# Layer 0's V phase: a block's row sums issued between the product G and its low part gl on VectorE

## The chip, the core and the metric

The kernel runs on one core of a Trainium2 chip. The metric is the device time of one launch in microseconds (us), taken as the median of several runs. TensorE (PE) multiplies matrices, with its weight loads shown as PEld; VectorE is DVE, ScalarE is ACT, GpSimd is POOL, and SyncE (SP) only issues transfers here.

## The reference

Two layers of a diffusion trunk over 256 context tokens and 256 latent tokens of width 1024. Each layer is a mixer (attention in layer 0, pooling and a recurrence in layer 1) followed by a PEER expert block. What matters here is the last lines of that block:

```python
def peer_ffn(h, wq, subkeys, u, v):
    ...
        eidx = jnp.take_along_axis(cidx, pos, axis=-1)
        g = jax.nn.softmax(top_s, axis=-1)
        act = jax.nn.gelu(jnp.einsum('td,thkd->thk', xc, u[eidx]).astype(jnp.float32), approximate=False)
        coef = (g * act).astype(xc.dtype)
        return jnp.einsum('thk,thkd->td', coef, v[eidx])
```

Each token chooses 8 heads x 16 experts = 128 rows of `v` out of 16384 and adds them up with its own weights.

## The kernel before

The kernel does not gather the rows for most tokens. It multiplies densely: the 16384 experts are 128 blocks of 128, the routing weights stand in a table `Wd` that is zero for experts not chosen, and the activations of all experts stand in `Gd`. The **V phase** of layer 0 is the loop `for j in range(NK)` (128 blocks) in `peer`. For block j it does this:

- SP fetches the block's 128x1024 rows of `v` into `wr` (4 buffers), the activations into `gr` (3 buffers), and every 8th block the weights of 8 blocks at once into `wb` (1536 KB, 2 buffers).
- `load_split` cuts `wr` into a rounded high part `whi` (ACT, L364) and the rest `wlo` (DVE, L365), 3 buffers each.
- DVE multiplies weights and activations to `G` (L1107, 128x384, 2 buffers). `split` makes the high part `gh` on ACT (L352) and the low part `gl` on DVE (L353), which reads `G` and `gh`. There are 3 buffers of each.
- PE adds three products (gh·whi, gl·whi, gh·wlo) for each of 8 column pieces into `y` (L1167): 24 matmuls of 384 columns.

Only 384 of the 512 tokens go this way in layer 0. The last 128 tokens go through `sparse`: POOL gathers, for each of their 128 choices, one row of `v` per token (128x1024, L1004) and one activation per token (L1009), into a ring of 10 row buffers, and DVE adds the row times its weight into `ysp` (L1024). Below, one such addition is a **row sum**. `sparse` is a generator; the loop over blocks advances it, by the `while done < ...` lines, so that the 128 row sums spread over the blocks 15 to 119: mostly one in a block, two in 23 of them.

DVE and POOL run in the order in which the code is written (`manual_schedule`). The orders of PE, ACT and SP come from a scheduler that plans each instruction by its own estimate of when the inputs are ready.

Of the kernel before, what the change touches and what calls it, by code (L numbers as in the profile page):

```python
# [21 lines left out]
P = 128  # L22
# [19 lines left out]
S0 = 14  # L42
S1 = 119
# [66 lines left out]
class Trunk:  # L110
# [918 lines left out]
    def peer(self, l, t0, extra=None):  # L1029
        nc, a = self.nc, self.a  # L1030
        n = T - t0
        nd = n if l else n - P
        Wd = self.dram.tile([nd // TG, P, NK, TG], F32, name=f"Wd{l}")
        Gd = self.Gd[l]
        with ExitStack() as es:
            ps = self.pool(es, f"psU{l}", 2, PSUM)
            rp = self.pool(es, f"route{l}")
            if l:
                hq = self.pool(es, "hq", side="right")
                h = [hq.tile([P, C, n], F32R, name=f"h{x}") for x in range(2)]  # L1040
            else:
                h = self.hf
            r = self.routing(l, ps, rp, h, n, Wd)
            if l == 0:
                xt = [self.new_tot() for _ in range(2)]
                self.sx = {"w": xt[0][:, :P], "g": xt[0][:, P:], "e": xt[1][:, :P].bitcast(U32),
                           "v": xt[1][:, P:].bitcast(U32)}
                self.tok = rp.tile([P, 1], F32, name="tok")
                nc.gpsimd.iota(self.tok, pattern=[[0, 1]], base=0, channel_multiplier=1,
                               allow_small_or_imprecise_dtypes=True)  # L1050
            next(r)
            if extra:
                self.mp = rp
                self.cb = rp.tile([P, 2, D], F32, tag="skey", name="cb")
                self.mod_load()
            es.enter_context(self.tc.manual_schedule(engines={mybir.EngineType.PE, mybir.EngineType.DVE}))
            total = (nd // P) * TOT + (n - nd) // P * TOTS
            st = [0.0, 0.0]
            pet = NK - (XU / 2 + 5 if l == 0 else 8)

            def pace(pe):
                st[1] += pe
                while st[0] * pet < total * st[1]:
                    c = next(r, None)
                    if c is None:
                        break
                    st[0] += c

            for j in range(NK):
                part = l == 0 and j < XU  # L1070
                self.u_step(ps, l, j, h, LC if part else 0, n, mid=lambda: pace(0.25 if part else 0.5))
                pace(0.25 if part else 0.5)
                if extra and j >= M0:
                    next(extra, None)
            for _ in r:
                pass
            if extra:
                for _ in extra:
                    pass
        es = ExitStack()  # L1080
        if l == 0:
            self.rec_alloc()
        ps = self.pool(es, f"psV{l}", 1, PSUM)
        vp = self.pool(es, f"vph{l}", 2)
        if l == 0:
            sp = self.sparse(vp)
            done = -1
            extra = self.v_extra()
        y = [ps.tile([P, n], F32, name=f"y{d}") for d in range(C)]
        last = []  # L1090
        vm = ExitStack()
        if l == 0:
            rc = self.rec_consts()
            vm.enter_context(self.tc.manual_schedule(engines={mybir.EngineType.DVE, mybir.EngineType.Pool}))
        for j in range(NK):
            if j % JB == 0:
                wb = vp.tile([P, nd // TG, JB, TG], F32, tag="wb", name="wb")
                nc.sync.dma_start(wb, Wd[:, :, j:j + JB, :].rearrange("g i j t -> i g j t"))
            g = vp.tile([P, nd], F32, tag="gr", name="gr", bufs=3)
            nc.sync.dma_start(g, Gd[j][:, :nd])  # L1100
            if l == 0 and j < XU:
                with self.tc.issue_after(self.gel.ins) if VG <= j < 6 else ExitStack():
                    nc.scalar.activation(g[:, :LC], g[:, :LC], AF.Gelu)
            with self.tc.issue_after(self.gel.ins) if j in VB else ExitStack():
                w = self.load_split(a["vT"][l, j])
            G = vp.tile([P, nd], F32, tag="G", name="G")
            nc.vector.tensor_tensor(G.rearrange("p (g t) -> p g t", t=TG), wb[:, :, j % JB, :],  # L1107
                                    g.rearrange("p (g t) -> p g t", t=TG), op=OP.mult)
            gh = vp.tile([P, nd], F32R, tag="gh", name="gh", bufs=3)
            gl = vp.tile([P, nd], F32R, tag="gl", name="gl", bufs=3)  # L1110
            if j < VD:
                nc.vector.tensor_copy(gh, G)
                nc.vector.tensor_tensor(gl, G, gh.bitcast(F32), op=OP.subtract)
            else:
                self.split(gh, gl, G)
            v = (w, gh, gl)
            if j < NK - KT:
                for d in range(C):
                    self.v_mm(y[d], v, d, 0, nd, j == 0)
            else:  # L1120
                last.append(v)
            if l == 0:
                if j in RC:
                    next(rc, None)
                if j == 40:
                    for d in range(C):
                        nc.vector.memset(y[d][:, nd:], 0.0)
                while done < (j - S0) * P / (S1 - S0):
                    if next(sp, 0) == 0:
                        break  # L1130
                    done += 1
                if j >= X0:
                    next(extra, None)
        if l == 0:
            for _ in sp:
                pass
            vm.close()
            for _ in extra:
                pass
        if l == 0:  # L1140
            self.bridge(es, y, last)
        else:
            self.tot = self.new_tot()
            for d in range(C):
                for v in last:
                    self.v_mm(y[d], v, d, 0, n)
                self.v_add(l, y[d], d, 1, 0)
                self.sq_acc(self.tot, d, LC, T)
            es.close()
# [444 lines left out]
```

## Time and profile before

| | |
|---|---|
| median of 3 runs | 2862.78 us (2859.86 to 2864.86) |
| the profiled execution | 2869.51 us, span 2867.7 us |
| mean granted TensorE clock | 0.966 of 2.4 GHz |
| PE busy | 2652.9 us, 93% of the span |
| DVE busy | 2098.2 us, 73% |
| bytes read and written by DMA | 631.58 MB, mean 220 GB/s |

The span runs from the first to the last instruction of the profiled execution; its own time is 1.8 us longer, and 6.7 us above the median of the runs. The blocks 15 to 119 of layer 0's V phase lie from about 1318 to 1824 us of the span. A busy share is a mean over stages that are limited by different things, so each stage has to be read by itself.

### The profile page before, as it was taken

Reading aid. Unit: us, or ns where it says so; the run is one execution under the profiler, and the core shown is the slowest. Engines: PE = TensorE matmul, PEld = TensorE weight load, DVE = VectorE, ACT = ScalarE, POOL = GpSimd, SP = SyncE. Lnnn points to the kernel's source line nnn. Section 1 sums busy time; section 2 is a strip of 40 time slices with the busy share of each in tenths; the row PEclk is TensorE's granted clock in tenths of the full one; section 3 lists DMA queues with packets and bytes.
Section 4 is the critical chain, followed back from the end, with each engine's and each line's share of the span. In section 5 each row is a group of like instructions: output and inputs, shape, how many; then the busy total and the mean of one; then the engine's idle time right before and its main releaser. Section 6 shows DMA issues by size and latency. Waiting matters only on the chain.

```text
span 2867.7 us, 45935 instructions
## 1 busy us (share of the span) xinstructions
PE 2652.9 (93%) x17403; PEld 2402.6 (84%) x17403; DVE 2098.2 (73%) x3697; ACT 1172.5 (41%) x1945; POOL 1285.1 (45%) x730
## 2 busy tenths in 40 slices
PE   8879999999899999999899998986999799999997
PEld 3667898987777777788888888976999799999997
DVE  5898764749958879226877777779839939677776
ACT  3444433433233333333333333354545445455544
POOL 3433430754444444445667665035387587600000
PEclk9989999999999999999999999998999999999999
DMA  7342262556547666667999998513477667898885
GB/s 258 125 133 74 95 211 81 192 190 242 197 169 269 228 227 221 196 235 259 316 324 340 342 322 305 190 50 111 157 217 242 210 209 240 289 302 294 293 287 167
DMA packets 296269, 631.58 MB, mean 220 GB/s; under 512 B 28480, under 2 KB 166384, under 8 KB 290416
## 3 DMA queue, kind: packets, MB, share of 16 engines
q1 hardware_dynamic: 226704, 468.03, 50.0%
q0 software_dynamic: 28768, 109.75, 10.3%
q10 hardware_dynamic: 40576, 50.87, 4.9%
q8 instruction: 136, 2.23, 0.3%
q14 instruction: 85, 0.70, 0.1%
HBM read 535.28 MB, written 93.33 MB: 219 GB/s over the span
## 4 chain that ended last, share of the span: by engine, by line
PE 47%; DVE 33%; issue 7%; DMA 6%; POOL 4%; ACT 3%; SPq 0%; ACTq 0%; DVEq 0%; POOLq 0%
PE y L1167 16%; PE pu L373 6%; PE pu L375 6%; PE pu L374 6%; DVE mj L166 4%; DVE A L973 3%; DVE B L975 3%; DVE B L976 3%; DVE wlo L365 3%; DVE B L974 2%; DVE ysp L1024 2%; POOL wlo L365 2%; PE pq L373 1%; PE pq L375 1%; PE pq L374 1%
## 5 line engine op out<-in xcount | busy, mean ns | idle before, releaser
L365 POOL TENSOR_TENSOR wlo<-wr,whi 128x1024 fp32r<-128x1024 f32 x306 | 800.7, 2623 | 729.3 <-ACT whi L364 591.9
L364 ACT ACTIVATE whi<-wr 128x1024 fp32r<-128x1024 f32 x575 | 609.1, 1060 | 937.6 <-PE pu L374 493.1
L1167 PE MATMUL y<-gh,whi 128*128 128x256 f32 (+1 forms) x2072 | 630.2, 310 | 41.4 <-ACT gh L352 40.1
L1167 PE MATMUL y<-gl,whi 128*128 128x256 f32 (+1 forms) x2072 | 642.6, 310 | 6.0 <-DVE gl L353 4.8
L1167 PE MATMUL y<-gh,wlo 128*128 128x256 f32 (+1 forms) x2072 | 637.7, 308 | 0.0
L365 DVE TENSOR_TENSOR wlo<-wr,whi 128x1024 fp32r<-128x1024 f32 x291 | 356.0, 1224 | 239.0 <-ACT whi L364 212.9
L1167 PEld LDWEIGHTS y<-gh,whi 128*128 128x128 f32 x2072 | 391.0, 190 | 52.6 <-ACT gh L352 50.5
L373 PE MATMUL pu<-hh,whi 128*128 128x512 f32 (+1 forms) x1024 | 395.7, 386 | 20.9 <-ACT gel L538 20.9
L1167 PEld LDWEIGHTS y<-gl,whi 128*128 128x128 f32 x2072 | 393.7, 190 | 15.3 <-DVE gl L353 12.8
L1167 PEld LDWEIGHTS y<-gh,wlo 128*128 128x128 f32 x2072 | 394.1, 190 | 0.0
L375 PE MATMUL pu<-hh,wlo 128*128 128x512 f32 (+1 forms) x1024 | 386.5, 377 | 3.7 <-POOL wlo L365 3.7
L374 PE MATMUL pu<-hl,whi 128*128 128x512 f32 (+1 forms) x1024 | 384.5, 375 | 0.0
L373 PE MATMUL pu<-h,whi 128*128 128x256 f32 x1024 | 296.1, 289 | 15.2 <-ACT whi L364 15.2
L375 PE MATMUL pu<-h,wlo 128*128 128x256 f32 x1024 | 290.6, 284 | 7.4 <-POOL wlo L365 7.4
L374 PE MATMUL pu<-h,whi 128*128 128x256 f32 x1024 | 289.6, 283 | 0.0
L373 PEld LDWEIGHTS pu<-hh,whi 128*128 128x128 f32 x1024 | 196.1, 191 | 53.4 <-ACT gel L538 22.7
L375 PEld LDWEIGHTS pu<-hh,wlo 128*128 128x128 f32 x1024 | 195.7, 191 | 41.0 <-POOL wlo L365 4.9
L374 PEld LDWEIGHTS pu<-hl,whi 128*128 128x128 f32 x1024 | 196.6, 192 | 31.8
L353 DVE TENSOR_TENSOR gl<-G,gh 128x384 fp32r<-128x384 f32 (+1 forms) x250 | 127.7, 511 | 119.6 <-ACT gh L352 119.6
L373 PEld LDWEIGHTS pu<-h,whi 128*128 128x128 f32 x1024 | 195.8, 191 | 15.4 <-ACT whi L364 15.4
L166 DVE SCALAR_TENSOR_TENSOR mj<-wm,cb 128x1024 bf16<-128x1024 f32 x128 | 206.6, 1614 | 1.0 <-DMA wm<-in_wmodT 0.8
L375 PEld LDWEIGHTS pu<-h,wlo 128*128 128x128 f32 x1024 | 195.2, 191 | 8.9 <-POOL wlo L365 8.9
(378 smaller groups left out, 4900.0 us busy)
## 6 DMA issues: line engine op xcount, KB each, us to landing
wr<-in_uT SPq DMA_DIRECT2D x278, 512.0 KB, 4.4
wr<-in_vT SPq DMA_DIRECT2D x256, 512.0 KB, 5.0
wm<-in_wmodT SPq DMA_DIRECT2D x80, 512.0 KB, 4.0
Wd<-stg POOLq DMA_DIRECT2D x40, 1024.0 KB, 7.0
Gd<-gel ACTq DMA_DIRECT2D x106, 256.0 KB, 2.4
wb<-Wd SPq DMA_DIRECT2D x16, 1536.0 KB, 12.5
gr<-Gd SPq DMA_DIRECT2D x128, 192.0 KB, 6.2
Gd<-gel ACTq DMA_DIRECT2D x172, 128.0 KB, 3.8
```

Source lines behind the costliest of these rows:

```text
L166: x = nc.vector.scalar_tensor_tensor(j, rs[i], 1.0, self.cb[:, s], op0=OP.mult, op1=OP.mult, accum_out=self.mv[l][n // C][:, n % C, s:s + 1])
L353: self.nc.vector.tensor_tensor(lo, x, hi.bitcast(F32), op=OP.subtract)
L364: nc.scalar.activation(hi, r, AF.Copy)
L365: (lo_engine or nc.vector).tensor_tensor(lo, r, hi.bitcast(F32), op=OP.subtract)
L373: nc.tensor.matmul(out, whi[:, s], hh[:, c, t0:t1], start=c == 0, stop=False)
L374: nc.tensor.matmul(out, whi[:, s], hl[:, c, t0:t1], start=False, stop=False)
L375: nc.tensor.matmul(out, wlo[:, s], hh[:, c, t0:t1], start=False, stop=c == C - 1)
L973: V.tensor_tensor(Av, io, x[0], op=OP.is_equal)
L974: V.tensor_tensor(Bv[1], io, x[1], op=OP.is_equal)
L975: V.tensor_tensor(Bv[0], Bv[1], x[2], op=OP.mult)
L976: V.tensor_tensor(Bv[1], Bv[1], x[3], op=OP.mult)
L1167: nc.tensor.matmul(y[:, n0:n1], w[:, s], g[:, n0:n1], start=first and x == 0, stop=False, skip_group_check=True)
```

## The change

The lines that advance the row sums move up. Before, a block's row sums were issued after `G`, `gl` and the block's matmuls. Now they are issued right after `G`, before `gh` and `gl`.

```diff
             G = vp.tile([P, nd], F32, tag="G", name="G")
             nc.vector.tensor_tensor(G.rearrange("p (g t) -> p g t", t=TG), wb[:, :, j % JB, :],
                                     g.rearrange("p (g t) -> p g t", t=TG), op=OP.mult)
+            while l == 0 and done < (j - S0) * P / (S1 - S0):
+                if next(sp, 0) == 0:
+                    break
+                done += 1
             gh = vp.tile([P, nd], F32R, tag="gh", name="gh", bufs=3)
             gl = vp.tile([P, nd], F32R, tag="gl", name="gl", bufs=3)
...
                 if j == 40:
                     for d in range(C):
                         nc.vector.memset(y[d][:, nd:], 0.0)
-                while done < (j - S0) * P / (S1 - S0):
-                    if next(sp, 0) == 0:
-                        break
-                    done += 1
                 if j >= X0:
                     next(extra, None)
```

The numbers of instructions stay the same on every engine. DVE's order for the blocks 59 and 60 of the loop before (G_14046 is block 59's product, G_14087 block 60's; `tot` is a small product that prepares the weights of eight row sums):

```order
L365 TENSOR_TENSOR wlo_14043<-wr_14040,whi_14042 128x1024
L1107 TENSOR_TENSOR G_14046<-wb_13910,gr_14038 128x384
L353 TENSOR_TENSOR gl_14049<-G_14046,gh_14048 128x384
L1024 SCALAR_TENSOR_TENSOR ysp_12095<-hl_12092,tot_4165,ysp_12095 128x1024
L365 TENSOR_TENSOR wlo_14084<-wr_14081,whi_14083 128x1024
L1107 TENSOR_TENSOR G_14087<-wb_13910,gr_14079 128x384
L353 TENSOR_TENSOR gl_14090<-G_14087,gh_14089 128x384
L1024 SCALAR_TENSOR_TENSOR ysp_12095<-hl_12092,tot_4165,ysp_12095 128x1024
L1019 TENSOR_TENSOR tot_4165<-tot_4165 128x8
L1024 SCALAR_TENSOR_TENSOR ysp_12095<-hl_12092,tot_4165,ysp_12095 128x1024
L365 TENSOR_TENSOR wlo_14129<-wr_14126,whi_14128 128x1024
```

The same two blocks on DVE now:

```order
L365 TENSOR_TENSOR wlo_14043<-wr_14040,whi_14042 128x1024
L1107 TENSOR_TENSOR G_14046<-wb_13910,gr_14038 128x384
L1024 SCALAR_TENSOR_TENSOR ysp_12067<-hl_12064,tot_4165,ysp_12067 128x1024
L353 TENSOR_TENSOR gl_14052<-G_14046,gh_14051 128x384
L365 TENSOR_TENSOR wlo_14084<-wr_14081,whi_14083 128x1024
L1107 TENSOR_TENSOR G_14087<-wb_13910,gr_14079 128x384
L1024 SCALAR_TENSOR_TENSOR ysp_12067<-hl_12064,tot_4165,ysp_12067 128x1024
L1019 TENSOR_TENSOR tot_4165<-tot_4165 128x8
L1024 SCALAR_TENSOR_TENSOR ysp_12067<-hl_12064,tot_4165,ysp_12067 128x1024
L353 TENSOR_TENSOR gl_14097<-G_14087,gh_14096 128x384
L365 TENSOR_TENSOR wlo_14129<-wr_14126,whi_14128 128x1024
```

The row sums moved from behind `gl` to in front of it; nothing else on DVE changed place.

The scheduler's plan for ACT changed with it. ACT's order around block 59 before (whi_14083 belongs to block 60, whi_14128 to block 61, gh_14048 to block 59):

```order
L352 ACTIVATE gh_14007<-G_14005 128x384
L364 ACTIVATE whi_14083<-wr_14081 128x1024
L352 ACTIVATE gh_14048<-G_14046 128x384
L364 ACTIVATE whi_14128<-wr_14126 128x1024
L352 ACTIVATE gh_14089<-G_14087 128x384
```

ACT's order there now (gh_14051 belongs to block 59, whi_14083 to block 60 as before):

```order
L364 ACTIVATE whi_14042<-wr_14040 128x1024
L352 ACTIVATE gh_14051<-G_14046 128x384
L364 ACTIVATE whi_14083<-wr_14081 128x1024
L352 ACTIVATE gh_14096<-G_14087 128x384
L364 ACTIVATE whi_14128<-wr_14126 128x1024
```

Before, the next block's `whi` stood ahead of this block's `gh` in 100 of the 105 blocks 15 to 119; now it does in 18 of them (26 to 31, 41 to 48, and four near 105).

PE's order at the start of block 79 before (gh_14890, gl_14891 and whi_14884 are block 79's; y0 to y7 are the column pieces):

```order
L1167 MATMUL y0_11482<-gh_14890,whi_14884 128x384
L1167 MATMUL y1_11483<-gh_14890,whi_14884 128x384
L1167 MATMUL y2_11484<-gh_14890,whi_14884 128x384
L1167 MATMUL y3_11485<-gh_14890,whi_14884 128x384
L1167 MATMUL y0_11482<-gl_14891,whi_14884 128x384
L1167 MATMUL y0_11482<-gh_14890,wlo_14885 128x384
```

PE's order there now (gh_14893 and gl_14894 are block 79's):

```order
L1167 MATMUL y0_11482<-gh_14893,whi_14884 128x384
L1167 MATMUL y0_11482<-gl_14894,whi_14884 128x384
L1167 MATMUL y0_11482<-gh_14893,wlo_14885 128x384
L1167 MATMUL y1_11483<-gh_14893,whi_14884 128x384
L1167 MATMUL y1_11483<-gl_14894,whi_14884 128x384
L1167 MATMUL y1_11483<-gh_14893,wlo_14885 128x384
```

Matmuls that need only `gh` were pulled ahead of the first one that needs `gl` in 33 of the 105 blocks; now they are in 6, and elsewhere `gl` is needed by the block's second matmul. SP's order of transfers differs only by swaps of neighbours. Outside the blocks 15 to 119 all orders are as before.

## Rows read from the trace of the kernel before

**Rows 1.** Page, part 4: shares of the chain that ended last, by engine.

```profile
PE 47%; DVE 33%; issue 7%; DMA 6%; POOL 4%; ACT 3%; SPq 0%; ACTq 0%; DVEq 0%; POOLq 0%
```

**Rows 2.** Stretch, us; PE, PEld, DVE, ACT, POOL busy; clock; DMA share; GB/s.

```profile
1318.00:1340.00 22.00, 18.41 (x96) 17.83 (x96) 12.82 (x18) 7.60 (x13) 9.44 (x8) 0.92 0.78 255
1340.00:1500.00 160.00, 147.36 (x806) 142.79 (x804) 128.07 (x180) 52.12 (x68) 106.85 (x81) 0.97 0.93 317
1500.00:1730.00 230.00, 211.48 (x1165) 202.22 (x1166) 180.14 (x213) 77.16 (x100) 155.84 (x119) 0.99 0.97 333
1730.00:1800.00 70.00, 62.30 (x332) 59.61 (x331) 54.98 (x62) 24.04 (x30) 30.17 (x18) 0.95 0.92 309
1800.00:1824.00 24.00, 23.67 (x136) 23.03 (x135) 20.06 (x25) 8.35 (x11) 0.00 (x0) 1.00 0.63 216
```

**Rows 3.** DVE's timeline: start, us, engine, line; a block with one sum, one with two.

```profile
1408.41 1.21 DVE L365 TENSOR_TENSOR wlo<-wr,whi 128x1024 fp32r<-128x1024 f32 x1
1409.55 0.55 DVE L1107 TENSOR_TENSOR G<-wb,gr 128x384 f32<-128x384 f32 x1
1410.75 0.60 DVE L353 TENSOR_TENSOR gl<-G,gh 128x384 fp32r<-128x384 f32 x1 [0.65 <-ACT gh L352]
1411.27 1.27 DVE L1024 SCALAR_TENSOR_TENSOR ysp<-hh,tot,ysp 128x1024 f32<-128x1024 f32 x1
1412.46 1.21 DVE L365 TENSOR_TENSOR wlo<-wr,whi 128x1024 fp32r<-128x1024 f32 x1
...
1415.32 2.59 DVE L1024 SCALAR_TENSOR_TENSOR ysp<-hh,tot,ysp 128x1024 f32<-128x1024 f32 x2
1417.83 1.22 DVE L365 TENSOR_TENSOR wlo<-wr,whi 128x1024 fp32r<-128x1024 f32 x1
```

**Rows 4.** Groups of DVE, 1318 to 1824: line, count, busy, mean ns, idle before.

```profile
L353 DVE TENSOR_TENSOR gl<-G,gh 128x384 fp32r<-128x384 f32 x105 | 64.2, 611 | 96.0 <-ACT gh L352 96.0
```

**Rows 5.** PE's timeline, 21 matmuls to the end of block 58; start of block 59.

```profile
1532.71 0.34 PE L1167 MATMUL y<-gh,whi 128*128 128x384 f32 x1
...
1536.17 0.34 PE L1167 MATMUL y<-gh,wlo 128*128 128x384 f32 x1
1537.62 0.44 PE L1167 MATMUL y<-gh,whi 128*128 128x384 f32 x1 [1.10 <-ACT gh L352]
```

**Rows 6.** ACT's timeline at the same place.

```profile
1530.93 0.53 ACT L352 ACTIVATE gh<-G 128x384 fp32r<-128x384 f32 x1 [2.53 <-DVE G L1107]
1536.09 1.06 ACT L364 ACTIVATE whi<-wr 128x1024 fp32r<-128x1024 f32 x1 [4.64 <-DMA wr<-in_vT]
1537.06 0.51 ACT L352 ACTIVATE gh<-G 128x384 fp32r<-128x384 f32 x1
```

**Rows 7.** Waits of ACT, 1318 to 1824: us in total, times, longest.

```profile
ACT whi L364 <- PE y L1167: 66.0, 63, 5.3
ACT whi L364 <- DMA wr<-in_vT: 64.7, 24, 6.9
```

**Rows 8.** DMA issues, 1318 to 1824: count, KB each, median us to landing.

```profile
wr<-in_vT SPq DMA_DIRECT2D x105, 512.0 KB, 5.6
gr<-Gd SPq DMA_DIRECT2D x105, 192.0 KB, 6.8
wb<-Wd SPq DMA_DIRECT2D x13, 1536.0 KB, 13.1
```

**Rows 9.** Short stretches, columns as in rows 2.

```profile
1534.00:1540.00 6.00, 4.75 (x26) 4.17 (x25) 3.30 (x5) 2.53 (x3) 2.75 (x4) 1.00 1.03 393
1544.00:1548.00 4.00, 3.56 (x20) 2.95 (x19) 3.35 (x5) 1.47 (x2) 3.39 (x3) 1.00 0.74 217
1560.00:1568.00 8.00, 8.00 (x48) 8.00 (x47) 7.20 (x8) 2.67 (x4) 5.18 (x5) 1.00 1.10 331
1604.00:1618.00 14.00, 12.73 (x73) 12.28 (x72) 11.17 (x15) 4.64 (x6) 10.28 (x9) 1.00 1.04 394
```

## The prediction

> **What bounds it now.** The page's chain gives DVE a third of the span [rows 1], although its busy share is lower than PE's; so there are stages in which DVE is waited for. I looked for them in the blocks with row sums, cut into stretches [rows 2]. PE is busy for 147.4 of 160 us, 211.5 of 230 and 62.3 of 70, and for 23.7 of 24 at the end, so it waits here and hardly there. The transfers stand at a share of 0.93, 0.97 and 0.92. DVE's timeline [rows 3] shows the order wlo, G, a hole of 0.65 us before gl, gl, the row sum, the next wlo. From wlo to wlo a block takes 1412.46 - 1408.41 = 4.05 us with one sum and 1417.83 - 1412.46 = 5.37 us with two. There are 82 blocks of the first kind and 23 of the second (counted from the loop's numbers), so DVE needs (82 x 4.05 + 23 x 5.37) / 105 = 4.34 us a block. PE goes from one matmul to the next in (1536.17 - 1532.71) / 20 = 0.173 us [rows 5], so a block's 24 cost it 4.15 us. DVE is therefore the slower of the two, and PE starts a block when DVE and ACT hand over its gh.
>
> A second limit lies close. Of the 96.0 us that DVE waits for gh before the 105 gl [rows 4], 105 x 0.65 = 68 us are the usual hole and 28 us are longer waits. One is block 59's: ACT stands for 4.64 us with block 60's whi, whose wr has not landed, and runs block 59's gh only after it [rows 6]; PE idles 1.10 us [rows 5]. ACT waited 24 times, 64.7 us, for a wr that was late [rows 7]. wr lands a median 5.6 us after its issue, the weights wb take 13.1 us [rows 8], and they come every 8 blocks, about as far apart as these stalls.
>
> **The change, part by part.**
>
> *DVE's hole.* The sum moves into the wait for gh. After G it runs for 1.27 us [rows 3], longer than the 0.65 us that gh needs, so gl finds gh ready. A block falls to 3.40 us with one sum, 4.72 with two, 3.69 on the average: below PE's 4.15. DVE is no longer the bound; by DVE and PE alone the stage would go at 4.15 us a block.
>
> *gl comes later.* After G, gl now starts 1.3 us on (one sum) or 2.6 us (two), not 0.65 us, and PE's second matmul wants it. This costs nothing if DVE runs ahead of PE. How far it can: whi has 3 buffers, so block j+1's whi starts when PE has ended block j-2. Then come whi 1.06 us, wlo 1.21, G 0.55, the sum 1.27, gl 0.60 [rows 3, 6]: 4.7 us, while PE has two blocks, 8.3 us, in hand. That leaves 3.6 us to spare, 2.3 with two sums. With that cover gone the price is the difference between sum and hole, 1.27 - 0.65 = 0.62 us, or 1.94 us with two: 0.91 us a block on the average.
>
> *ACT's new order.* gh of block j now stands ahead of whi of block j+1 in 87 of the 105 blocks (18 keep the old order instead of 100). A late wr then delays only the next block, and PE can finish the present one, 4.15 us of work, in the meantime. The 28 us of longer waits, over and above the hole, should mostly be covered. It adds no wait of its own: whi is queued behind gh, which waits for G, and G ends 1.3 us or more before the next wlo wants that whi; gh and whi together take 1.59 us [rows 6] while DVE does sum and gl, 1.87 us. I count it at nothing beyond what the next paragraph allows.
>
> *PE's new order and the swaps on SP.* The up to 4 matmuls of gh that ran ahead of gl covered at most 0.52 us in 33 blocks; with gl early they are not needed. SP swaps neighbours and POOL's order is the same; sums that run earlier only free row buffers sooner. The memsets of block 40 wait for PE either way. Nothing for these.
>
> *The transfers.* At 4.15 us a block they would have to bring the same bytes faster than now, and here I expect the new limit. The share in the three stretches makes 160 x 0.93 + 230 x 0.97 + 70 x 0.92 = 436 us of work in 460 us [rows 2]. How full can it get? Where a backlog certainly stands (a whi waiting for wr) the share is 1.03 or 1.04 at 393 and 394 GB/s; with wb under way it is 1.10 at only 331 GB/s; between them it falls to 0.74 at 217 GB/s for want of requests [rows 9]. So 0.97 was not full. The bounds: at 1.045, nearly the backlog level, the 436 us of work take 417 us, 43 us less than now. If the share gets to 0.97 everywhere and no higher, they take 450 us, 10 us less. I take 1.00, about halfway, because requests still come only as buffers free (4 wr, 3 gr) and a wb still goes ahead of a wr in one queue: 436 us, **24 us less**. PE's floor for the same stretches, (806 + 1165 + 332) x 0.173 = 398 us, lies below, so PE does not undo it. The Trainium skill's page "Perfetto Trace Analysis", section "Identifying the Most-Contended Engine", would have a DMA limit judged by bytes per second against the peak, not by occupancy; by that the 333 GB/s of the long stretch leave more room than its share of 0.97 does, and the sum would go to PE's floor. The rows with wb under way speak against it here, since there the engines are fuller at fewer bytes.
>
> *Elsewhere.* The first 22 us hold a wait for the first gathers, which stays. In the last 24 us PE is already busy 23.67 us: at most 0.3 us. Other stages keep their order.
>
> **Sum.** 24 us off the profiled execution's 2869.5 us is 2845.5 us; the runs' median lies 6.7 us below that execution, so I predict **2839 us** for the median.
>
> **Rivals.**
>
> *PE becomes the bound.* If the transfers follow, the three stretches take PE's 398 us and some 4 us for the memsets and the constants in between: 58 us less, 2805 us. For it speak the 393 GB/s: the 160 x 317 + 230 x 333 + 70 x 309 GB/s·us = 149 MB would take 379 us at that rate. Against it: wb's stretches do not reach it, and the backlog has to stand all the time. By the Trainium skill's "Perfetto Trace Analysis", section "Roofline", a core alone can draw up to about 430 GB/s, by which the bytes would take 346 us, less than PE; no stretch in these rows reaches that figure. Chance 0.10.
>
> *The transfers are at their limit already.* Then the longest stretch stays as it is and the others rise at most to its 0.97: 0 to 14 us, with 2853 us for the 10 us worked out above. For it speaks the DMA share itself and the late wr in rows 7; against it the dips to 0.74. Chance 0.27, about half of it within 0.2%.
>
> *Slower: gl comes late.* If wr is late by more than the 3.6 us to spare, DVE does not run ahead; after the landing PE then waits for whi, wlo, G, the sum and gl, where it used to start with gh. This costs 0.91 us at each of the 24 late wr, 22 us: 2885 us, if nothing is gained back. It decides once DVE's lead stays under a block through most of the stage. Against it: the same late wr holds up gh of the block before as well now, and that ends for most blocks. Chance 0.07.
>
> **The numbers.** The forecast (12 to 43 us gained) has 0.56. Faster by over 0.2% (5.7 us, about what a measurement of this kernel can tell from no change) takes the forecast, PE's bound and 0.12 of the limit case: 0.78. Within 0.2% lie 0.14 of the limit case and 0.01 of the late gl: 0.15. Slower: 0.07. The range goes from the 43 us of the full backlog, 2820, to 2864, a limit case without gain: about 0.08 lies below and 0.12 above. The forecast alone would span 2820 to 2851.
>
> **What would show it.** In the changed profile, DVE's gl should have lost its usual 0.65 us before gh: the 96 us should fall under 30. The time of a block of one sum should be set by PE, with DVE idle before wlo (waiting for whi, and whi for PE or for wr). PE's waits for gl may grow while those for gh vanish. The DMA share should rise to about 1.00 between 1340 and the end of the gathers, and SP's wr should land later than 5.6 us. The step to doubt most is how full the transfers can get: if the share stays at 0.97 or less with PE idle as before, the limit rival holds; if PE is busy throughout and wr lands early, PE's bound does. If PE waits for gl in most blocks, the slower case holds.

## The result, and the profile after

The changed kernel takes 2830.11 us (median of 4 runs, 2823.82 to 2838.03) against 2863.82 us before (4 runs, 2859.86 to 2868.17). The ratio is 0.9884, with a 95% interval of 0.9868 to 0.9901: 33.7 us less, by the interval 28 to 38 us. The forecast was 24 us less, 2839 us, in a range of 2820 to 2864.

The profiled execution of the changed kernel took 2831.33 us, 38.2 us less than the one of before, so it shows a little more than the medians do. All of it lies in the stage with row sums. From the start of block 15's G to that of block 119's G the kernel before takes from 1318.0 to 1822.7 us, 504.7 us; the changed one from 1317.5 to 1780.5 us, 463.0 us. Four of these 41.7 us are given back at once: from block 119 to block 127 G takes 29.2 us before and 33.3 us after. Before, DVE was behind PE and caught up there; now it is ahead, and PE sets the pace.

Part 4 of the page now gives the chain to PE, where DVE had a third of it [rows 1]:

```profile
PE 59%; DVE 26%; DMA 4%; issue 4%; ACT 3%; POOL 2%; SPq 0%; DVEq 0%; ACTq 0%; POOLq 0%
```

The stretches of the changed kernel that answer to rows 2 (us; busy us of PE, PEld, DVE, ACT and POOL with their instructions; granted clock, DMA share, GB/s):

```profile
1317.00:1340.00 23.00, 21.11 (x117) 20.54 (x116) 16.22 (x22) 8.11 (x13) 11.63 (x10) 0.97 0.92 300
1340.00:1460.00 120.00, 116.91 (x656) 115.86 (x656) 107.09 (x158) 43.42 (x57) 88.54 (x67) 0.98 1.00 349
1460.00:1700.00 240.00, 233.42 (x1317) 231.95 (x1316) 198.44 (x240) 85.59 (x111) 173.19 (x133) 0.98 1.02 360
1700.00:1760.00 60.00, 54.78 (x298) 52.65 (x297) 51.81 (x57) 19.95 (x26) 24.94 (x16) 0.97 0.94 322
1760.00:1786.00 26.00, 26.00 (x152) 26.00 (x151) 21.71 (x27) 10.06 (x13) 0.00 (x0) 1.00 0.68 232
```

PE is busy 97% of the two long stretches, and the transfers run at a share of 1.00 and 1.02 at the same time. Which of the two holds the stage is taken up below, with the runs without row gathers.

DVE's timeline of the changed kernel, to be read beside rows 3:

```profile
1604.05 1.22 DVE L365 TENSOR_TENSOR wlo<-wr,whi 128x1024 fp32r<-128x1024 f32 x1
1605.19 0.55 DVE L1107 TENSOR_TENSOR G<-wb,gr 128x384 f32<-128x384 f32 x1
1605.66 1.28 DVE L1024 SCALAR_TENSOR_TENSOR ysp<-hh,tot,ysp 128x1024 f32<-128x1024 f32 x1
1606.85 0.55 DVE L353 TENSOR_TENSOR gl<-G,gh 128x384 fp32r<-128x384 f32 x1
1608.20 1.23 DVE L365 TENSOR_TENSOR wlo<-wr,whi 128x1024 fp32r<-128x1024 f32 x1 [0.80 <-ACT whi L364]
```

gl follows the sum without a hole. In this block the hole is now ahead of wlo, where DVE waits for whi. From wlo to wlo is 1608.20 - 1604.05 = 4.15 us, PE's time for a block; DVE's own work, without the new wait of 0.80 us, is 3.35 us. Not every block looks like this: over the 81 blocks with one sum the median from wlo to wlo is 3.61 us and the mean 4.22, where they were 4.06 and 4.60 before. DVE does most blocks at its own pace and stands still in fewer of them, for longer.

The waits of DVE, PE and ACT in the changed kernel, 1317 to 1782 us (us in total, times, longest), beside rows 4 and 7:

```profile
DVE wlo L365 <- ACT whi L364: 38.1, 36, 6.5
DVE gl L353 <- ACT gh L352: 10.8, 7, 6.2
```

```profile
PE y L1167 <- ACT gh L352: 13.0, 7, 4.7
PE y L1167 <- DVE gl L353: 3.4, 4, 1.8
```

PE's waits before, 1318 to 1824 us:

```profile
PE y L1167 <- ACT gh L352: 37.4, 28, 5.1
PE y L1167 <- DVE gl L353: 4.1, 7, 1.8
```

ACT's waits in the changed kernel:

```profile
ACT whi L364 <- PE y L1167: 42.0, 41, 3.1
ACT whi L364 <- DMA wr<-in_vT: 25.6, 15, 3.9
```

DVE's wait for gh fell from 96.0 us to 10.8, PE's from 37.4 to 13.0; ACT's wait for late wr fell from 64.7 to 25.6. Yet a wr lands later than before, in the changed kernel's issues between 1318 and 1790 us (count, KB, median us to landing), beside rows 8:

```profile
wr<-in_vT SPq DMA_DIRECT2D x106, 512.0 KB, 7.1
```

So the single transfer did not become quicker; its delay is waited for less. That DVE and PE have more work in hand is the likely reason.

### The profile page after: what moved, and what is told of

It is laid out like the page before. It is cut to its first block, busy times and chain, and to the rows that moved or that the text cites. A ratio compares the mean times of both kernels' runs of the same rounds, so it can differ in the third digit from the quotient of the medians.

```text
span 2829.5 us, 46000 instructions
## 1 busy us (share of the span) xinstructions
PE 2642.1 (93%) x17403; PEld 2404.2 (85%) x17403; DVE 2092.1 (74%) x3697; ACT 1170.3 (41%) x1945; POOL 1284.5 (45%) x730
## 4 chain that ended last, share of the span: by engine, by line
PE 59%; DVE 26%; DMA 4%; issue 4%; ACT 3%; POOL 2%; SPq 0%; DVEq 0%; ACTq 0%; POOLq 0%
PE y L1167 24%; PE pu L373 8%; PE pu L375 7%; PE pu L374 7%; DVE mj L166 3%; DVE B L974 2%; DVE B L976 2%; POOL wlo L365 2%; DVE B L975 2%; DMA gr<-Gd 2%; PE pq L373 1%; PE pq L375 1%; PE pq L374 1%; DVE A L973 1%; PE pw L957 1%
## 5 line engine op out<-in xcount | busy, mean ns | idle before, releaser
L352 ACT ACTIVATE gh<-G 128x384 fp32r<-128x384 f32 (+1 forms) x250 | 115.5, 462 | 213.0 <-DVE G L1107 173.7
```

The costliest lines, as they stand in the source:

```text
L352: self.nc.scalar.activation(hi, x, AF.Copy)
```

## The experiments

The question is which part made the gain: the sum in DVE's hole, or ACT's new order, or the sums (and the gathers that follow them) being earlier; and what limits the stage now. Each run is given by its median against that of the kernel before in the same comparison, and by the time from the start of block 15's G to that of block 119's in its profile (504.7 us before, 463.0 us after).

**ACT's order alone (e1).** The kernel before, its DVE order untouched; ACT follows the code from block 24 on, so that gh stands ahead of the next whi:

```diff
+            if l == 0 and j == 24:
+                vm.close()
+                vm.enter_context(self.tc.manual_schedule(engines={mybir.EngineType.DVE, mybir.EngineType.Pool,
+                                                                  mybir.EngineType.Activation}))
             if j % JB == 0:
```

> The kernel before, with ACT kept in the order of the code from block 24 on, so that a block's gh stands ahead of the next block's whi (8 of the blocks 15 to 119 keep the old order); DVE's order is that of before. If the sum in DVE's hole makes the gain, DVE still needs 4.05 us for a block of one sum and 5.37 for one of two, and only the longer waits for gh can go (28 us of DVE's waits, part of them hidden): 0 to 12 us faster, some 2855 us. If ACT's new order makes the gain, most of the 34 us come here too: some 2832 us.

Measured: 2846.32 against 2865.57 us, ratio 0.9925 (0.9899 to 0.9951); the stage takes 486.6 us. That is 19 us, more than the 12 I allowed and less than the rival's 34. DVE's waits, 1314 to 1802 us:

```profile
DVE gl L353 <- ACT gh L352: 76.1, 103, 6.3
```

Of 103 waits, 103 x 0.65 = 67 us are the usual hole, which is all there; the longer waits shrank from 28 us to 9, about as much as the stage gained. In the timeline of before 15 waits for gh are longer than 0.8 us. Six of them (13 us beyond the hole) stand behind a whi whose transfer is late, five (8 us) behind a whi that waits for PE to free its buffer, and four (7 us) in the first blocks behind late activations gr. In this run the first two kinds are gone and the third stays. Most of the 66.0 us that whi waits for PE before [rows 7] held up no gl.

**The sums alone (e2).** The changed kernel with ACT's order of before: from block 24 on the next block's whi is issued ahead of gh, its wlo stays where it was.

```diff
-                w = self.load_split(a["vT"][l, j])
+                w = self.load_low(*ahead) if ahead else self.load_split(a["vT"][l, j])
+            ahead = None
...
+            if l == 0 and 24 <= j < NK - 1:
+                ahead = self.load_high(a["vT"][l, j + 1])
             gh = vp.tile([P, nd], F32R, tag="gh", name="gh", bufs=3)
```

> The changed kernel's order on DVE (sums between G and gl), with ACT's order of before put back from block 24 on: the next block's whi ahead of this block's gh (96 of 105 blocks). If the sum in the hole makes the gain, most of it stays: 20 to 34 us faster than before, 2830 to 2845 us, with late wr still holding up gh. If ACT's order makes it, this stands at the time of before, 2855 to 2864 us.

Measured: 2837.32 against 2865.57 us, ratio 0.9898 (0.9864 to 0.9932); stage 469.0 us. Most of the gain is here without ACT's new order. DVE's waits, 1312 to 1782 us:

```profile
DVE gl L353 <- ACT gh L352: 40.0, 47, 3.7
```

The usual hole is gone from more than half of the blocks. 36 of the waits left are 0.6 us on the average; of the eleven longer than 0.8 us ten stand behind a whi that waits for a late wr. The two parts alone take 504.7 - 486.6 = 18.1 and 504.7 - 469.0 = 35.7 us off the stage, 53.8 together, where the change takes off 41.7: they overlap. The intervals of this run and of the changed kernel overlap, so what ACT's order adds once the sums are moved (7 us by the medians) is not shown to differ from nothing.

**Half of each sum (e9).** DVE's work cut by other means, with the order of before:

```diff
-                V.scalar_tensor_tensor(ys, v, c, ys, op0=OP.mult, op1=OP.add)
+                V.scalar_tensor_tensor(ys[:, :D // 2], v[:, :D // 2], c, ys[:, :D // 2], op0=OP.mult, op1=OP.add)
```

> The kernel before with each row sum over 512 of the 1024 columns (the other half of the sums is left out; the gathers still bring whole rows). DVE's order and hole stay, ACT's order is nearly that of before (90 of 105 blocks), but a sum takes some 0.64 us less, as much as the hole. If DVE's pace was what the change took away, this gains about as much as the run with the sums moved and ACT's old order (28 us): 2830 to 2845 us. If only filling the hole or ACT's order helps, it stays within 8 us of the kernel before.

Measured: 2840.0 against 2863.77 us, ratio 0.9909 (0.9878 to 0.994); stage 477.7 us. A sum takes 0.74 us there, 0.54 less and not 0.64, and 24 us go. The hole is still in place (DVE waits 116.7 us for gh, 104 times). It is thus DVE's time for a block that counted; filling the hole is one way to shorten it.

**Sums ahead of G (e5).** The `while` lines moved up once more, ahead of the line that makes `G`.

> The row sums moved still further up, ahead of G: DVE's order is wlo, sums, G, gl. The sums come as early as in the changed kernel, but G, gh and gl stand next to each other again, so the 0.65 us hole is back in each block, and the scheduler gives ACT its order of before (102 of 105 blocks). If the filled hole and ACT's order make the gain, this is within 8 us of the kernel before, some 2860 us. If the gain came from the sums and the gathers that follow them being earlier, it is near the changed kernel's 2830 us.

Measured: 2857.14 us (10 runs) against 2862.71 (17 runs), ratio 0.999 (0.9973 to 1.0006): no difference that can be told. Its profiled stage takes 491.3 us, 13 less than that of the kernel before, but half of this comes from the profiled execution of before, whose 2869.5 us lie 5.7 us over its kernel's median of 2863.82. The same excess is in every gain that is given here in stage times. DVE's waits, 1314 to 1816 us:

```profile
DVE gl L353 <- ACT gh L352: 85.9, 107, 5.8
```

The hole is back in each block. The sums stand as early in the order as in the changed kernel, so their being early is not what makes the 34 us; by the interval it is worth 8 us at most.

**Without most row gathers (e3 and e4).** In the changed kernel and in that of before, only the first 10 gathers of rows are made:

```diff
-            if k < P:
+            if k < len(ring):
                 G.indirect_dma_start(out=ring[k % len(ring)], out_offset=None, in_=vf,
```

> The changed kernel without the gathers of rows after the first 10 (the sums run on, over the rows that are there): 118 of 128 gathers of 512 KB are left out. If the transfers are the limit now, PE's idle time between 1317 and 1760 us (17 us) and the clock lost with it go: 12 to 20 us faster than the changed kernel, some 2814 us. If PE is the limit already, it stays within 5 us of the changed kernel.

> The kernel before without the same 118 gathers. If DVE's order set the pace, a block still takes 4.34 us on the average, 4.05 with one sum and 5.37 with two, and only what late transfers cost goes: 20 to 40 us faster than before, 2825 to 2845 us, and slower than the changed kernel without the gathers by about 105 x 0.19 = 20 us. If the transfers set the pace before, the stage falls to PE's 4.15 us a block, some 2805 us, and the two kernels without gathers are equal.

Measured, against 2865.57 us: changed kernel without rows 2803.16 us, ratio 0.978 (0.9746 to 0.9814), stage 438.7 us; kernel before without rows 2837.51 us, ratio 0.9893 (0.9859 to 0.9928), stage 475.8 us. The stretches of the blocks 24 to 95 and 96 to 105, from G to G, in the changed kernel and then in the same kernel without the gathers (columns as in rows 2):

```profile
1358.87:1668.45 309.58, 304.62 (x1733) 302.90 (x1732) 268.84 (x353) 110.78 (x144) 231.64 (x176) 0.99 1.03 363
1668.45:1726.47 58.02, 49.49 (x251) 47.14 (x250) 40.98 (x44) 18.13 (x23) 29.92 (x22) 0.91 0.89 296
```

```profile
1352.61:1656.70 304.09, 300.67 (x1730) 299.27 (x1729) 268.63 (x353) 113.60 (x144) 90.03 (x73) 1.00 0.70 218
1656.70:1699.78 43.08, 42.15 (x242) 41.58 (x241) 41.94 (x45) 17.95 (x23) 8.40 (x3) 1.00 0.81 257
```

Without the gathers the changed kernel is 27 us faster, more than the 12 to 20 I expected; their bytes, their packets and POOL's work for them go together in this run. The rows show where the time was. In the 72 blocks 24 to 95 the changed kernel's transfers stand at a share of 1.03, and it still needs only 309.6 us where 304.1 are needed without the gathers. PE is busy for 304.6 of them: there PE sets the pace, and not the transfers. The ten blocks 96 to 105 take 58.0 us against 43.1. These are 15 of the 24.3 us between the two stages (463.0 and 438.7); 4 more lie in the blocks 15 to 23. The share in the ten blocks is 0.89, and the change gains next to nothing there (58.6 us before). Near them the kernel also fetches the first weights of layer 1 (`in_rw_in`, in the code from block 98 on), and ACT splits them (L1287) ahead of a gh. ACT's wait for them in the changed kernel, 1317 to 1782 us:

```profile
ACT whi L1287 <- DMA wr<-in_rw_in: 14.3, 3, 8.9
```

It is 5.7 us without the gathers. Behind the longest one DVE's gl waits 6.20 us for gh and PE 4.71 us. So what the gathers still cost shows mostly as single late transfers in a few blocks. This is read from the trace: no run moves these loads.

DVE's waits in the kernel before without the gathers, 1316 to 1794 us:

```profile
DVE gl L353 <- ACT gh L352: 75.2, 105, 3.4
```

It stays at DVE's pace, its hole intact, 34 us slower than the changed kernel without them, where 20 were expected. A block takes 475.8 / 104 = 4.58 us there and not the expected 4.34: DVE has other work in some blocks (one with constants for layer 1 takes 10.45 us, block 40 with its memsets 8.50), and three operations beside POOL's L1290 take some 2 us longer (a gl 2.41 us in place of 0.56). The change gains 34 us with the gathers and 34 without, and the gathers cost 28 us before the change (2865.57 - 2837.51) and 27 after it (30 by the ratios). That the transfers took something off the gain is therefore not shown.

**wb in pieces (e6).** The changed kernel, with the next 8 blocks' weights fetched 3 of 24 parts at a time:

```diff
+            if nxt is not None:
+                g0, g1, j0 = j % JB * 3, j % JB * 3 + 3, j // JB * JB + JB
+                nc.sync.dma_start(nxt[:, g0:g1], Wd[g0:g1, :, j0:j0 + JB, :].rearrange("g i j t -> i g j t"))
```

> The changed kernel with layer 0's table of weights fetched in 8 pieces of 192 KB, one per block, in place of 1536 KB at once (from block 16 on). If the late wr come from standing behind wb in SP's queue, wr lands sooner and up to 10 us go, some 2820 us. If the sum of the bytes is what limits, the time stays within 4 us of the changed kernel.

Measured: 2829.15 against 2862.71 us, ratio 0.988 (0.9866 to 0.9895): as the changed kernel. SP's order puts several pieces next to each other, so the transfer is spread over some blocks only. From 1460 to 1700 us the share is 1.02 at 360 GB/s, as in the changed kernel, and a wr lands a median 8.0 us after its issue, not sooner than the 7.1 there.

**The second sum of a block behind gl (e7).** In the 23 blocks with two sums one stands ahead of gl and one behind. The edit is against the kernel before, whose `while` lines behind the matmuls stay and make the second sum:

```diff
+            one = True
+            while l == 0 and one and done < (j - S0) * P / (S1 - S0):
+                if next(sp, 0) == 0:
+                    break
+                done += 1
+                one = j < S0 + 2
```

> The changed kernel with only one row sum of a block between G and gl; the second one of 23 blocks stands behind gl again. If a late gl costs PE time, this gives back up to 23 x 1.3 = 30 us at most, more likely 2 to 5 us. If DVE's lead covers it, as forecast, the time stays within 3 us of the changed kernel.

Measured: 2830.39 against 2862.71 us, ratio 0.9884 (0.987 to 0.9898): as the changed kernel. A gl that is 1.3 us later in 23 blocks costs nothing that can be told. By an estimate from the two intervals a difference of some 6 us could hide here: the 30 us are ruled out, the 2 to 5 us are not.

**Both orders everywhere (e8).** The changed kernel with e1's lines.

> The changed kernel with ACT kept in the order of the code from block 24 on: the 18 blocks in which the next block's whi still stood ahead of gh are gone. If that order still costs, in proportion to the e1 run's 18 us for about 92 blocks, some 3 us go: 2827 us. If DVE's lead covers it, no change.

Measured: 2831.48 against 2862.71 us, ratio 0.9901 (0.9878 to 0.9925): no gain over the changed kernel that can be told, and an interval too wide for the 3 us.

## Why the prediction was right, and what it had wrong

*DVE's hole.* Right. DVE's cycle was the pace: cutting it in two quite different ways (e2, e9) gave 28 and 24 us, and moving the sums without filling the hole (e5) gave nothing that can be told. The wait for gh fell under the 30 us that were named. DVE's 4.34 us a block were too low, as they leave out its other work and the longer waits: without the gathers it was 4.58, and with them the kernel before took 504.7 / 104 = 4.85. The sign that was named for the new state, DVE idle before wlo, shows in 36 waits and not in most blocks.

*gl later, at no cost.* Right as far as the runs can tell. PE waits no longer for gl than before (3.4 us against 4.1; its weight loads 6.5 against 11.2), and with an earlier gl in 23 blocks (e7) the time is the same. The slower rival did not happen.

*ACT's order.* That gh ahead of the next whi frees the longer waits was right, but I gave late wr as their cause. It was the larger one; whi waiting for PE was a second. The order alone is worth 19 us as long as DVE sets the pace (e1), and nothing that can be told on top of the moved sums (e2, e8).

*The transfers as the new limit.* The time fell into the range, but this step is only partly borne out, and its term, 24 us for the three stretches, was mis-sized: they went from 460 us to 420. I put the share at 1.00; between 1340 and 1760 us the trace gives 120 x 1.00, 240 x 1.02 and 60 x 0.94, 421 us in 420, so that was met. But the work itself, 436 us of share, was read off the kernel before and taken as fixed, and it was not. The stretches up to the end of the gathers, before and after:

```profile
1318.00:1800.00 482.00, 439.54 (x2395) 422.45 (x2395) 376.01 (x472) 160.91 (x208) 302.30 (x224) 0.98 0.94 321
1317.00:1760.00 443.00, 426.22 (x2383) 421.00 (x2382) 373.56 (x474) 157.07 (x207) 298.31 (x224) 0.98 1.00 349
```

Both bring 155 MB. Divided by the share, that is 341 GB/s before and 349 after, and these 2% are worth some 10 us of 436. Some 4 us more come from the first stretch, which I left as it was: it does 23 x 0.92 = 21 us of the transfers' work where it did 22 x 0.78 = 17. The 2 us that are left of the 16 are within the rounding of the shares. The first stretch and the one after the gathers give back 1 and 2 us, so 37 of the 38 us between the profiled executions are accounted for; the medians differ by 33.7, because the profiled execution of before lies 5.7 us over its median.

The mechanism behind the term fared worse than its size. In the blocks 24 to 95 the share was full and PE set the pace all the same (309.6 us, 304.1 without the gathers). What the transfers still cost lies mostly in the ten blocks 96 to 105, at a share of 0.89, and it is no more than they cost before the change (27 and 28 us). A sum over the busy share does not describe this; that it came within 9 us of the median is in part luck.

*PE as the bound.* That rival's 2805 us is what e3 reached, 2803 us, with most of the gathers gone. With them its mechanism holds in the blocks 24 to 95 and not in the ten blocks behind them, and the kernel stays 27 us above it. The ceiling for a core alone that the Trainium skill's page "Perfetto Trace Analysis" gives in its section "Roofline", about 120% of 358 GB/s, by an estimate some 430 GB/s, was not needed for it and did not show: over 240 us the highest rate found is 368 GB/s (e2, 1452 to 1692 us), over 8 us 406 GB/s (the changed kernel, 1729 to 1737 us).

*The limit at 0.97.* Wrong: the share rose above it.

Left open is why a full share moves more bytes in the changed kernel. The other runs agree with it: over their stages, rate divided by share is 339 to 344 GB/s where DVE's hole is in place (e5 322 / 0.95, e1 327 / 0.95, e9 333 / 0.97) and 347 to 349 where the sums fill it (e2 340 / 0.98, e8 340 / 0.98, e7 342 / 0.98); the rounding of a share alone is 2 GB/s. e6 shows that this way of cutting wb does not raise it; what it is in the mix of transfers was not tried.

## What to carry to other kernels

When an engine works in program order and each round has a short wait for another engine in it, independent work of about that length belongs into the wait, and not ahead of it or behind it; whether it pays depends on this engine's time for a round, hole included, being longer than the next engine's. Look on the other engines at what the scheduler does with the change: taking an instruction that waits for a buffer or a transfer from in front of a short one that others wait for was worth 19 us here by itself. And do not take the busy share of the transfers as work that stays fixed, or a full share as the limit: the same 155 MB were 482 x 0.94 = 453 us of share before and 443 after. Whether transfers hold a kernel is better seen by leaving some of them out, before the change and after it.

## What was not expected of the hardware

The busy share of the 16 DMA engines does not end at 1: it stood at 1.02 for 240 us, and at 1.10 with 331 GB/s for 8 us [rows 9]. A share of 0.97 over 230 us therefore left room for 8% more bytes per second (333 to 360 GB/s), in the changed kernel with the same transfers. Nor did a full share hold PE up: at 1.03 over the 310 us of the blocks 24 to 95, PE was busy for 98% of the time.
